# One step of a hybrid trunk: where the scan output's and the attention's tiles lie in memory

## The chip, the cores and the metric

The kernel runs on one core of a Trainium2 chip. The metric is device time of one execution in microseconds; lower is better. The core has five engines with a queue of instructions each: TensorE (PE, its weight loads PEld), VectorE (DVE), ScalarE (ACT), GpSimd (POOL) and SyncE (SP, which only issues DMAs here). Each engine works through its own queue in order and waits at an instruction until what that needs is there.

## What is computed

Two layers work on 640 tokens (512 latent, 128 context) of width 1024. A layer has one input projection whose columns go to three groups of heads: a diagonal complex scan with a gated unit (A), latent attention (B) and a gated mixing of chunks (C). Their outputs are normed, joined and projected; then comes a gated convolutional feed-forward part. The modulation of a layer is a product of SiLU(cond) with a matrix w_mod. The parts that matter here:

```python
def mixer_ssm(u, h0_re, h0_im, p):
    ...
    y = jax.nn.gelu(y).astype(u.dtype)
    y = y * jax.nn.sigmoid(y @ p['ssm_w_glu'])
...
def block_attention(q, k, v):
    ...
        s = jnp.einsum('bqhd,bkhd->bhqk', q_blk, k).astype(F32) * ATTN_SCALE
        w = jax.nn.softmax(s, axis=-1).astype(v.dtype)
        return jnp.einsum('bhqk,bkhd->bqhd', w, v)
...
def trunk_layer(x, mod, p, ctx):
    ...
    y_a, h_re, h_im = mixer_ssm(u_ssm, zeros, zeros, p)
    ...
    y_b = block_attention(q, k, v)
    y_c = mixer_gmlp(uv, p)
    x = x + gate1 * merge_heads(y_a, y_b, y_c, p['w_out_norm'], p['w_out'])
    x = x + gate2 * conv_ffn(modulate(x, shift2, scale2), p)
```

## The kernel before

All activations are held transposed (features on partitions, 642 columns: 512 latent, two of padding, 128 context). Products that need full precision are made as three products of split operands (`mm3`, lines 141 to 143).

The program is written in one order, layer by layer, and a planner at build time sets the order of the instructions in each engine's queue: an instruction written later may be put ahead of one written earlier where the planner's clock says that it is ready first. Tiles come from pools. A pool takes a stretch of the on-chip memory from one of two ends (`self.sides`, `sa` and `sb`; layer 1 swaps left and right), stacked on the pools that are open on that side, and gives it back when it closes; the program adds the waits between the users of one stretch. The order of the pools is so that of the opening and closing calls in `mixers`.

In `mixers` (from line 835) a layer's first half is written in this order. The first two blocks of the input projection give `uT`, the scan's input, in the pool `ssm` on side `sb`; it goes to DRAM and comes back as `U`. The function `scans` (line 926) runs four quarters (`ssm_quarter`), each of which writes a part of the scan's result to DRAM (`Yd`, line 781), stores the states (`ssm_states`) and calls `ssm_output`. In layer 1 `scans` is called before the chunk mixing, in layer 0 behind it. Then the pools `vt` and `prj` open on side `sa`; the rest of the projection, keys, values and queries are made there, with norms on VectorE (`key_norms`, `query_norms`; line 1163 on, line 1174 scales the queries, lines 1184 to 1189 turn those of the latent tokens in scratch tiles of `prj`). Then `prj` and `ssm` close, `yb` opens on `sa`, and `att` on `sb`, and `attention` runs.

`ssm_output` (lines 794 to 830) reads `Yd` back into `yT` with 16 DMAs, half of them from SP and half from GpSimd, and the gate's weights into `wg`; makes the GELU of two halves in `ga` and `gb` (lines 811 to 815), the gate's product (`glu`, line 824) and its sigmoid in `th`, and writes `yA` (line 830), which the merge reads later. All its tiles take over tags of the pool `ssm` (`yT` that of `U`, `wg` that of `tp`, and so on).

`attention` fills constant rows on GpSimd (lines 1214 to 1216), then handles the context heads in a pool of their own, `actx` (lines 1297 to 1344: transposes `ctr` into `qc` and `kc`, products `cmx` and maxima `nm`, scores `cs`, exponentials `Pc`, sums `co`). Among these stand `turn(0)` and `turn(1)`, which transpose the first two latent heads into `qh`, `ql`, `kh`, `kl` (lines 1223 to 1239, in `att`), and their `maxima` (`mx`, `nml`). Behind `actx` the pool `at2` opens, with the tiles `P` of the latent heads' exponentials (line 1271). Four pairs of heads follow. Between them `fill` issues steps of `mod_blocks` (lines 232 to 272): a block of w_mod is loaded from SP into one of three buffers `raw` (line 258) and multiplied (`mod`, line 261).

Of the kernel before, what the change touches and what calls it, by code (L numbers as in the profile page):

```python
# [23 lines left out]
NT = 642  # L24
# [23 lines left out]
class Trunk:  # L48
# [745 lines left out]
    def ssm_output(self, l, pool, yA):  # L794
# [3 lines left out]
        y = pool.tile([128, 2, 8, NC], F32, name=self.uid("yT"), tag="uT", bufs=1)  # L798
# [4 lines left out]
        wg = pool.tile([128, 2, 256], F32, name=self.uid("wg"), tag="tp", bufs=1)  # L803
        nc.sync.dma_start(out=wg, in_=I["ssm_w_glu"][l].rearrange("(t p) n -> p t n", t=2))
        g = [pool.tile([128, NT], F32, name=self.uid("gl"), tag=tg, bufs=1) for tg in ("E", "R")]
        for t in range(2):
            yv = y[:, t].rearrange("p i k -> p (i k)")
            nc.gpsimd.memset(g[t][:, 512:CX], 0.0)
            a = pool.tile([128, n], F32, name=self.uid("ga"), tag="m1", bufs=1)
            b = pool.tile([128, n], F32, name=self.uid("gb"), tag="m2", bufs=1)  # L810
            nc.scalar.activation(a, yv, AF.Square)
            V.tensor_scalar(a, a, 0.044715, 1.0, op0=OP.mult, op1=OP.add)
            V.tensor_tensor(a, a, yv, op=OP.mult)
            nc.scalar.activation(b, a, AF.Tanh, scale=math.sqrt(2.0 / math.pi))
            V.scalar_tensor_tensor(a, b, 1.0, yv, op0=OP.add, op1=OP.mult)
            av = a.rearrange("p (i k) -> p k i", i=8)
            for k0, k1, c in ((0, 64, 0), (65, 81, CX)):
                o = g[t][:, c:c + 8 * (k1 - k0)].rearrange("p (k i) -> p k i", i=8)
                nc.scalar.activation(o, av[:, k0:k1], AF.Copy, scale=0.5)
        for m in range(2):  # L820
# [5 lines left out]
            for s, (lo, hi) in enumerate(((0, 320), (320, NT))):  # L826
                th = pool.tile([128, 322], F32, name=self.uid("th"), tag="H", bufs=1)
# [5 lines left out]
    def mixers(self, l, M, n1, N, hh, hl, fill):  # L833
# [94 lines left out]
        def scans(tables):  # L928
            hq = ssm.tile([128, 2, 2, 2, NS], F32, name=self.uid("hq"), tag="hq")
            for q in range(4):  # L930
                self.ssm_quarter(l, q, ssm, tables or self.ssm_load(l, q, ssm), U, st, hq)
                tables = None
            self.ssm_states(l, st)
            self.ssm_output(l, ssm, yA)
# [16 lines left out]
        if l == 0:  # L951
# [4 lines left out]
            scans(None)  # L956

# [111 lines left out]
        ssm_ctx.close()  # L1069
# [4 lines left out]
        with ExitStack() as es:  # L1074
            at = es.enter_context(tc.tile_pool(name=f"att{l}", bufs=1, side=sb))
# [115 lines left out]
    def attention(self, l, M, yb, at, es, qs, ks, Vt, yB, yA, yc, ssc, fill):  # L1191
# [105 lines left out]
        with self.tc.tile_pool(name=f"actx{l}", bufs=1, side=self.sides[1]) as cx:  # L1297
# [458 lines left out]
```

## Time and profile before

| | us |
|---|---|
| median of 3 runs | 1825.25 |
| lowest and highest | 1825.23 and 1832.4 |
| the profiled execution | 1826.58 |
| its span, first to last instruction | 1824.8 |
| TensorE busy | 1694.3 (93%) |
| VectorE busy | 1156.8 (63%) |
| ScalarE busy | 679.8 (37%) |
| GpSimd busy | 312.8 (17%) |

The profile is of one execution. The table of stretches tells which engine is full where. The timeline lists an engine's instructions with their start, length, line, tiles, and in square brackets how long the engine had sat idle before and what ended that. Layer 0's first half ends at some 390 us and layer 1's at some 1280 us; what lies between and behind is the feed-forward part, in which TensorE has hardly a gap.

### The profile page before, as it was taken

Reading aid. Unit: us, or ns where it says so; the run is one execution under the profiler, and the core shown is the slowest. Engines: PE = TensorE matmul, PEld = TensorE weight load, DVE = VectorE, ACT = ScalarE, POOL = GpSimd, SP = SyncE. Lnnn points to the kernel's source line nnn. Section 1 sums busy time; section 2 is a strip of 40 time slices with the busy share of each in tenths; the row PEclk is TensorE's granted clock in tenths of the full one; section 3 lists DMA queues with packets and bytes.
Section 4 is the critical chain, followed back from the end, with each engine's and each line's share of the span. In section 5 each row is a group of like instructions: output and inputs, shape, how many; then the busy total and the mean of one; then the engine's idle time right before and its main releaser. Section 6 shows DMA issues by size and latency. Waiting matters only on the chain.

```text
span 1824.8 us, 28970 instructions
## 1 busy us (share of the span) xinstructions
PE 1694.3 (93%) x11248; PEld 1512.6 (83%) x11248; DVE 1156.8 (63%) x2421; ACT 679.8 (37%) x1210; POOL 312.8 (17%) x738
## 2 busy tenths in 40 slices
PE   5878889999989999999999888999989999999998
PEld 3767755468889999999999876455989999999998
DVE  6887875667674646556477568566786464555564
ACT  4334454433452414224244346343344232332241
POOL 2886200000086060540000120000000000000000
PEclk7889789899899999999999978999989999999999
DMA  9265453301443523234132633540223131331221
GB/s 281 84 174 148 124 162 123 110 15 56 129 137 118 170 56 116 59 94 116 35 90 67 164 105 107 167 133 1 70 70 93 36 104 47 93 92 36 82 82 58
DMA packets 217577, 182.48 MB, mean 100 GB/s; under 512 B 33438, under 2 KB 202204, under 8 KB 217440
## 3 DMA queue, kind: packets, MB, share of 16 engines
q1 hardware_dynamic: 194736, 154.33, 28.2%
q0 software_dynamic: 8272, 23.87, 4.4%
q10 hardware_dynamic: 14432, 2.44, 0.7%
q8 instruction: 89, 1.46, 0.3%
q14 instruction: 48, 0.39, 0.1%
HBM read 161.94 MB, written 18.64 MB: 99 GB/s over the span
## 4 chain that ended last, share of the span: by engine, by line
PE 75%; DVE 10%; DMA 7%; ACT 4%; POOL 2%; issue 2%; ACTq 1%; SPq 0%; DVEq 0%; POOLq 0%
PE up L141 11%; PE up L143 11%; PE up L142 11%; PE dn L142 6%; PE dn L141 6%; PE dn L143 6%; PE o L1287 3%; PE mod L261 2%; DMA raw<-w_mod 2%; PE wo L141 1%; PE wo L143 1%; PE wo L142 1%; DMA raw<-ffn_w_up 1%; PE s L1267 1%; PE win L141 1%
## 5 line engine op out<-in xcount | busy, mean ns | idle before, releaser
L141 PE MATMUL up<-hh,whi 128*128 128x322 f32 x1408 | 435.6, 315 | 8.8 <-ACT hh L357 7.9
L143 PE MATMUL up<-hh,wlo 128*128 128x322 f32 x1408 | 440.9, 314 | 1.1 <-DVE wlo L118 1.0
L142 PE MATMUL up<-hl,whi 128*128 128x322 f32 x1408 | 439.7, 313 | 1.6 <-DVE hl L358 1.5
L141 PEld LDWEIGHTS up<-hh,whi 128*128 128x128 f32 x1408 | 266.1, 191 | 14.3 <-ACT hh L357 7.2
L142 PEld LDWEIGHTS up<-hl,whi 128*128 128x128 f32 x1408 | 268.8, 191 | 2.6 <-DVE hl L358 2.6
L143 PEld LDWEIGHTS up<-hh,wlo 128*128 128x128 f32 x1408 | 267.9, 190 | 2.9 <-DVE wlo L118 1.9
L118 DVE TENSOR_TENSOR wlo<-raw,whi 128x1024 fp32r<-128x1024 f32 (+1 forms) x116 | 146.7, 1266 | 142.2 <-ACT whi L117 141.0
L142 PE MATMUL dn<-glo,dh 128*128 128x322 f32 (+1 forms) x704 | 218.5, 312 | 0.2 <-DVE glo L118 0.2
L143 PE MATMUL dn<-gh,dl 128*128 128x322 f32 (+1 forms) x704 | 217.9, 311 | 0.0
L141 PE MATMUL dn<-gh,dh 128*128 128x322 f32 (+1 forms) x704 | 209.4, 312 | 4.5 <-DVE xT L1501 2.9
L1501 DVE SCALAR_TENSOR_TENSOR xT<-dn,mod,xT 128x320 f32<-128x320 f32 (+2 forms) x288 | 112.2, 435 | 129.5 <-PE dn L143 129.3
L117 ACT CAST whi<-raw 128x1024 fp32r<-128x1024 f32 (+1 forms) x116 | 120.5, 1040 | 151.1 <-PE up L142 56.8
L1532 ACT ACTIVATE cv<-up,prm,cw 128x321 f32<-128x321 f32 x88 | 54.3, 619 | 252.5 <-PE up L143 252.3
L141 PEld LDWEIGHTS dn<-gh,dh 128*128 128x128 f32 x704 | 131.0, 190 | 5.3 <-DVE xT L1501 3.1
L142 PEld LDWEIGHTS dn<-glo,dh 128*128 128x128 f32 x704 | 133.2, 189 | 0.5 <-DVE glo L118 0.5
L143 PEld LDWEIGHTS dn<-gh,dl 128*128 128x128 f32 x704 | 133.5, 190 | 0.0
L1533 DVE SCALAR_TENSOR_TENSOR cv<-up,cw,cv 128x320 f32<-128x320 f32 x88 | 48.3, 549 | 67.5 <-ACT cv L1532 67.5
L261 PE MATMUL mod<-raw,sT 128*32 128x256 f32 x768 | 64.5, 431 | 27.1 <-DMA raw<-w_mod 24.8
L118 DVE TENSOR_TENSOR dl<-raw,dh 128x1024 fp32r<-128x1024 f32 x44 | 54.0, 1227 | 45.8 <-ACT dh L117 45.6
L117 ACT CAST dh<-raw 128x1024 fp32r<-128x1024 f32 x44 | 46.1, 1047 | 56.8 <-DMA raw<-ffn_w_down 50.1
L261 PEld LDWEIGHTS mod<-raw,sT 128*32 128x32 f32 x768 | 19.5, 114 | 57.5 <-DMA raw<-w_mod 29.2
L1250 DVE TENSOR_REDUCE nml<-mx 128x1 f32<-128x640 f32 x64 | 50.9, 820 | 24.0 <-PE mx L1248 23.7
(472 smaller groups left out, 3422.5 us busy)
## 6 DMA issues: line engine op xcount, KB each, us to landing
raw<-w_mod SPq DMA_DIRECT2D x96, 512.0 KB, 4.6
raw<-ffn_w_up SPq DMA_DIRECT2D x88, 512.0 KB, 4.1
raw<-ffn_w_down SPq DMA_DIRECT2D x44, 512.0 KB, 3.5
raw<-w_in SPq DMA_DIRECT2D x10, 512.0 KB, 5.7
we<-WEd POOLq DMA_DIRECT2D x8, 512.0 KB, 4.1
qt<-Qd POOLq DMA_DIRECT2D x8, 512.0 KB, 5.1
raw<-w_out SPq DMA_DIRECT2D x16, 256.0 KB, 5.1
raw<-w_out SPq DMA_DIRECT2D x8, 512.0 KB, 3.4
```

Of the source, the lines that this page charges most:

```text
L117: self.nc.scalar.copy(hi, raw)
L118: self.nc.vector.tensor_tensor(lo, raw, hi.bitcast(F32), op=OP.subtract)
L141: mm(ps, wh, xh, start=start, stop=False)
L142: mm(ps, wh, xl, start=False, stop=False)
L143: mm(ps, wl, xh, start=False, stop=stop)
L261: nc.tensor.matmul(ps[j * 32:j * 32 + 32, c0:c0 + 256], self.sT[:, k0 + j, :], rv[:, j, :], start=k0 == 0, stop=k0 == 4)
L1250: V.tensor_reduce(nm[:, tt:tt + 1], pb[:, :, :320], axis=AX.XY, op=OP.max, negate=True)
L1267: mm(ps, kh[i][:, kc_], qh[i], start=True, stop=False)
L1287: mm(pb[i * 64:(i + 1) * 64, 0], Vt[:, kt, 2 * p + i], Ps[i][kt], start=kt == 0, stop=kt == 4)
L1501: self.nc.vector.scalar_tensor_tensor(self.xT[:, m, a:b], po[:, a - lo:b - lo], self.modcol(l, gi, m, c), self.xT[:, m, a:b], op0=OP.mult, ...
L1532: A.activation(z[:, 0:321], po[:, 0:321], AF.Identity, bias=b, scale=c1)
L1533: V.scalar_tensor_tensor(z[:, 1:321], po[:, 0:320], c0, z[:, 1:321], op0=OP.mult, op1=OP.add)
```

## The change

The pool `ssm` closes at the scan's last output, before `vt` opens, not before the attention. `ssm_output` is taken out of `scans` and gets a pool of its own, `so`, on the same side, with tags of its own; its tile `gb` goes and the tanh is made in place in `ga`. In layer 1 it is thereby written behind the chunk mixing. The pools `att` and `actx` open on side `sa`, on top of `yb`; `at2` stays on `sb`.

```diff
@@ ssm_output
-        y = pool.tile([128, 2, 8, NC], F32, name=self.uid("yT"), tag="uT", bufs=1)
+        y = pool.tile([128, 2, 8, NC], F32, name=self.uid("yT"), tag="yT", bufs=1)
...
-        wg = pool.tile([128, 2, 256], F32, name=self.uid("wg"), tag="tp", bufs=1)
+        wg = pool.tile([128, 2, 256], F32, name=self.uid("wg"), tag="wg", bufs=1)
...
-        g = [pool.tile([128, NT], F32, name=self.uid("gl"), tag=tg, bufs=1) for tg in ("E", "R")]
+        g = [pool.tile([128, NT], F32, name=self.uid("gl"), tag=tg, bufs=1) for tg in ("g0", "g1")]
...
-            a = pool.tile([128, n], F32, name=self.uid("ga"), tag="m1", bufs=1)
-            b = pool.tile([128, n], F32, name=self.uid("gb"), tag="m2", bufs=1)
+            a = pool.tile([128, n], F32, name=self.uid("ga"), tag="ga", bufs=1)
...
-            nc.scalar.activation(b, a, AF.Tanh, scale=math.sqrt(2.0 / math.pi))
-            V.scalar_tensor_tensor(a, b, 1.0, yv, op0=OP.add, op1=OP.mult)
+            nc.scalar.activation(a, a, AF.Tanh, scale=math.sqrt(2.0 / math.pi))
+            V.scalar_tensor_tensor(a, a, 1.0, yv, op0=OP.add, op1=OP.mult)
...
-                th = pool.tile([128, 322], F32, name=self.uid("th"), tag="H", bufs=1)
+                th = pool.tile([128, 322], F32, name=self.uid("th"), tag="th", bufs=1)
@@ mixers
             self.ssm_states(l, st)
-            self.ssm_output(l, ssm, yA)
...
             scans(None)
+        ssm_ctx.close()
+        with tc.tile_pool(name=f"so{l}", bufs=1, side=sb) as so:
+            self.ssm_output(l, so, yA)
...
         prj.close()
-        ssm_ctx.close()
...
-            at = es.enter_context(tc.tile_pool(name=f"att{l}", bufs=1, side=sb))
+            at = es.enter_context(tc.tile_pool(name=f"att{l}", bufs=1, side=sa))
@@ attention
-        with self.tc.tile_pool(name=f"actx{l}", bufs=1, side=self.sides[1]) as cx:
+        with self.tc.tile_pool(name=f"actx{l}", bufs=1, side=self.sides[0]) as cx:
```

## Rows read from the trace of the kernel before

**Rows 1.** The page: busy share of TensorE; the chain that ended last, by engine.

```profile
PE 1694.3 (93%) x11248; PEld 1512.6 (83%) x11248; DVE 1156.8 (63%) x2421; ACT 679.8 (37%) x1210; POOL 312.8 (17%) x738
PE 75%; DVE 10%; DMA 7%; ACT 4%; POOL 2%; issue 2%; ACTq 1%; SPq 0%; DVEq 0%; POOLq 0%
```

**Rows 2.** Busy time by stretch: stretch, length, each engine's busy us, granted clock, DMA.

```profile
240.00:250.00 10.00, 6.29 (x58) 3.26 (x57) 9.65 (x25) 2.06 (x5) 0.00 (x0) 0.96 0.51 163
245.00:340.00 95.00, 84.64 (x566) 46.29 (x567) 58.57 (x107) 43.09 (x83) 3.27 (x6) 0.94 0.57 181
280.00:290.00 10.00, 9.04 (x64) 5.64 (x63) 7.45 (x20) 7.63 (x17) 0.00 (x0) 1.00 0.03 6
1107.00:1137.00 30.00, 23.60 (x155) 18.69 (x154) 28.45 (x73) 16.34 (x24) 2.94 (x6) 0.82 0.46 150
1160.00:1170.00 10.00, 9.65 (x68) 7.17 (x71) 8.15 (x23) 7.53 (x18) 0.00 (x0) 1.00 0.18 55
```

**Rows 3.** Timeline of GpSimd: start, length, line, tiles, idle before and its releaser.

```profile
250.67 0.52 POOL L1214 MEMSET ql<- 1x512 f32 x1 [31.83 <-DVE yA L830]
...
1075.15 1.05 POOL L800 DMA_DIRECT2D yT<-Yd  x2 [3.11 <-DMA Yd<-ys]
```

**Rows 4.** Timeline of VectorE, layer 0.

```profile
249.99 0.49 DVE L830 TENSOR_TENSOR yA<-th,gl 128x322 f32<-128x322 f32 x1
...
251.77 0.69 DVE L1189 TENSOR_TENSOR qs<-qx,qx 128x512 f32<-128x512 f32 x1
```

**Rows 5.** Timeline of ScalarE, layer 0.

```profile
250.65 1.26 ACT L1305 ACTIVATE qc<-ctr,qg 96x512 f32<-96x512 f32 x2 [1.87 <-DVE yA L830]
251.80 1.25 ACT L1236 ACTIVATE kh<-kt,kg 96x512 fp32r<-96x512 f32 x2
```

**Rows 6.** Timeline of TensorE, layer 0.

```profile
247.48 0.64 PE L261 MATMUL mod<-raw,sT 128*32 128x256 f32 x8 [2.79 <-DMA raw<-w_mod]
249.05 0.93 PE L261 MATMUL mod<-raw,sT 128*32 128x256 f32 x8 [0.93 <-DMA raw<-w_mod]
...
253.44 1.09 PE L147 MATMUL ctr<-ident,ks 128*96 128x128 f32 x4
...
256.73 2.05 PE L1313 MATMUL cmx<-kc,qc 96*128 96x128 f32 x16
...
333.39 0.64 PE L261 MATMUL mod<-raw,sT 128*32 128x256 f32 x8 [2.13 <-DMA raw<-w_mod]
```

**Rows 7.** Timeline of VectorE, layer 1.

```profile
1106.48 0.61 DVE L1154 TENSOR_SCALAR ms<-ms 128x48 f32<-128x48 f32 x1
...
1107.74 0.58 DVE L104 TENSOR_SCALAR rs_y<-rs_sh 128x48 int32<-128x48 int32 x1
...
1121.25 0.75 DVE L1237 SCALAR_TENSOR_TENSOR kl<-kt,kg,kh 96x512 fp32r<-96x512 f32 x1
...
1123.65 0.34 DVE L1237 SCALAR_TENSOR_TENSOR kl<-kt,kg,kh 96x128 fp32r<-96x128 f32 x1
...
1125.11 0.18 DVE L1154 TENSOR_SCALAR ms<-ms 128x32 f32<-128x32 f32 x1
...
1135.96 0.68 DVE L1189 TENSOR_TENSOR qs<-qx,qx 128x512 f32<-128x512 f32 x1
```

**Rows 8.** Timeline of ScalarE, layer 1.

```profile
1077.95 0.75 ACT L811 ACTIVATE ga<-yT 128x648 f32<-128x648 f32 x1 [2.02 <-DMA yT<-Yd]
...
1136.94 0.62 ACT L1354 ACTIVATE ac<-yA 128x512 f32<-128x512 f32 x1
...
1160.99 1.08 ACT L1271 ACTIVATE P<-s 128x512 f32<-128x512 f32 x2
```

**Rows 9.** Timeline of TensorE, layer 1.

```profile
1082.98 0.80 PE L1036 MATMUL kv<-whi,ckh 128*128 128x512 f32 x1 [3.19 <-ACT sq L980]
...
1213.76 0.64 PE L261 MATMUL mod<-raw,sT 128*32 128x256 f32 x8 [3.08 <-DMA raw<-w_mod]
```

**Rows 10.** Instructions on the tile `yT`: its DMAs, from issue to landing.

```profile
DMA to landing us min/median/max: 1.9/4.2/5.5
```

## The prediction

> **What bounds the kernel now.** I read the page first: TensorE is busy for 93% of the span and carries 75% of the chain that ended last [rows 1]. So an edit that adds no matmul can only win TensorE's idle time and the time it runs at the lower clock. The stretches come next [rows 2]: in layer 0 from 245 to 340 us TensorE is busy for 84.64 of 95.00 us (granted clock 0.94), and in layer 1 from 1107 to 1137 us for 23.60 of 30.00 us (0.82) while VectorE is busy for 28.45 of 30.00. That last row says who is late there: VectorE, with the norms of the queries and keys. In layer 0 the tightest ten microseconds, 240 to 250, hold 9.65 us of VectorE and 6.29 us of TensorE.
>
> Then I ask what the attention waits for. GpSimd's fill of `ql` (line 1214) reads nothing, yet it sat idle for 31.83 us until line 830, the last step of the scan output [rows 3]. `ql` belongs to the pool `att`, laid over the memory of the pool `ssm`, and line 830 reads two tiles of `ssm`. The first copy into `qc` (line 1305, pool `actx`) also starts at 250.65, right behind line 830 at 249.99 plus 0.49 us [rows 4, 5]. So the first instructions of a pool wait for the last user of the whole pool that lay there. The same is seen on the other side: line 1354 writes `ac` (pool `yb`, over the closed projection pool `prj`) at 1136.94, just behind line 1189 at 1135.96 plus 0.68 us, the last that touches `prj` [rows 7, 8].
>
> **The change part by part.** From the tile shapes in the code, in bytes of one partition: `prj` has about 31,000, `yb` 17,500, `att` 23,600. On the new side `att` stands on `yb` and covers 17,500 to 41,100, so it lies over `prj`; `actx` starts at 41,100 and lies over nothing recent. `at2` drops to the bottom of the old side, over `ssm` and the new pool `so`, both done by then. So the edit exchanges waits: `actx` loses its wait for line 830; `att` exchanges line 830 for line 1189; `at2` loses its wait for the end of the context heads; the scan output's tiles wait for the whole of `ssm`.
>
> (1) `actx`, layer 0. Its 16 transposes, copies and the `cmx` products need only the context rows, but were held to 250.65. TensorE meanwhile waits 2.79 and 0.93 us for blocks of w_mod, at 247.48 and 249.05 [rows 6]: 3.72 us together. What can fill them is the four `ctr` transposes at 253.44 (1.09 us), their twins (not shown, four more of the same) and the `cmx` products at 256.73 (2.05 us): 4.2 us of work. The queue is fixed when the program is built, so not every hole is met; I take -3.0, ends -3.7 and 0. In layer 1 the context rows themselves come late, so nothing there. The load of `kc`'s one-hot rows (line 1299) stands in SP's queue among the w_mod blocks and is set free with `actx`; it can only stop holding those behind it.
>
> (2) `att`, layer 0. Its first copy `kh` moves from 251.80 [rows 5] to behind 251.77 plus 0.69, which is 252.46 [rows 4]: 0.7 us later. The turned queries need line 1189 anyway. I take 0, ends 0 and +0.7. GpSimd has nothing queued behind its fills.
>
> (3) `att`, layer 1. Before, the copies `kl` (line 1237) were made in the middle of VectorE's chain: 0.75 and 0.34 us for a head [rows 7], 2.2 us for two. Behind line 1189 they no longer delay the norms. The six fills leave this chain too: beside them line 1154 and the two steps behind it took 0.61, 0.58 and 0.58 us (the first and the last are shown), against 0.18 for the same line later [rows 7], which is 1.2 us in all. So line 1189 ends up to 3.4 us earlier. Given back: the two long `kh` copies, 1.25 us for two as in layer 0 [rows 5], now stand behind the gate. I take -2.0; ends -3.4 (all kept) and +3.4 (chain not shortened, and `kh` with both heads' `kl` behind it: 1.25 + 2.2).
>
> (4) `at2`. In layer 1 the first exponential into `P` started at 1160.99 [rows 8], when the context heads were through. With `P` free earlier, the scores of the first pair and the context heads can fill one another's gaps. TensorE's idle there is 0.96 us (280 to 290) and 0.35 us (1160 to 1170) [rows 2]. I take -1.0, ends -1.3 and 0.
>
> (5) The pool `so`. Sixteen DMAs bring `yT`, eight from SP, eight from GpSimd, 0.53 us of issue each on the latter. Before, most of them started as soon as `U` was read; only two on GpSimd waited for the last store, up to 1075.15 in layer 1 [rows 3]. Now all wait for it. The half that line 811 reads first is four issues on each queue: 1075.2 + 2.1 = 1077.3, and with the median landing of 4.2 us [rows 10] it is there at 1081.5, where line 811 started at 1077.95 after waiting 2.02 us [rows 8]. So up to 3.5 us later. Behind line 811 on ScalarE stand the copies that release TensorE, which already idles 3.19 us at 1082.98 [rows 9]. Should the planner put those copies ahead of line 811, the wait of 2.02 us disappears instead. In layer 0 the same sum gives 0.6 us, with other work on ScalarE over it. I take 0; ends -2.0 and +4.1. Also on SP's queue the w_glu load and the first w_mod blocks come after the eight loads; those blocks lay unused until 243 in layer 0, so that costs nothing.
>
> A page has another price for the landing. The Trainium skill, "DMA: Bandwidth & Descriptors", section "Anatomy of one DMA — SWDGE (gpsimd) path", gives about 2.0 us of fixed cost for a transfer; by that estimate the upper end of (5) would be +1.4 in layer 1 and the range would lose some 2 us above. The trace says 1.9 at least and 4.2 in the middle [rows 10], so the page's figure is its best case and I keep mine.
>
> (6) What is late next: the stream of w_mod blocks that fills the attention. At its end TensorE already waits 2.13 us in layer 0 [rows 6] and 3.08 us in layer 1 [rows 9] for the last block. A gain made early in the attention lets the stream move up only as far as its three buffers are freed earlier. I give back +2.0 of the 6.0; ends 0 and +5.2 (both waits grow by all that was won ahead of them, at most the sum of the two waits).
>
> Arithmetic, tanh in place and the smaller tiles: same instructions with the same shapes, cost nothing. Sum: -3.0 + 0 - 2.0 - 1.0 + 0 + 2.0 = -4.0 us. The profiled execution took 1826.58 us (span 1824.8 and 1.78 around it), so 1822.6; it stands 1.3 above the median of 1825.25, so the prediction is 1821.3, rounded 1821.
>
> **The rivals.** *The gate only moves.* The attention of a latent head cannot begin before the queries are turned (line 1189) in either kernel, so the wait that goes was never the last one, and w_mod sets the pace. For it: VectorE is full in both stretches [rows 2] and in layer 0 line 1189 ends 2 us after line 830 [rows 4]. Against it: the 3.72 us of holes in layer 0. Time: 1825, no change (0 to -1).
>
> *The holes close altogether.* The planner lays out the whole attention anew, and context work fills most of the stalls: of the 10.36 us idle in 245 to 340 and the 6.40 us in 1107 to 1137 [rows 2], plus the 3.19 and 2.02 us around line 811. If half of the first two and all of (5)'s gain are won: -8.4 - 2.0 = about -10, 1815. Against it: w_mod's waits at the end stay.
>
> *Slower, by the pool `so`.* Line 811 stays at its place in ScalarE's queue and the data come 3.5 us later; TensorE's idle of 3.19 us at 1082.98 grows by that, and the scan output's last steps (0.49 us for each line 830 [rows 4], some 3.3 us in all with line 829) slide into the stretch in which VectorE has 1.55 us to spare. That is 3.5 + 3.3 = +6.8 us, against it (1) and (4) at half, -2 and -0.5, with 2.5 returned by w_mod: about +6.8, 1832. It decides from the point where the first half of `yT` lands later than about 1079.7, when line 811 would end in its old place plus its own slack, and where the planner did not see it.
>
> **How the numbers follow.** Forecast 0.45 (its own range 1817 to 1824.5), gate only moves 0.20, holes close 0.18, slower 0.17. Differences of 0.5%, 9.1 us, are about what a measurement of this kernel can tell from no change: below 1816.1 counts as faster, above 1834.4 as slower. Faster: the holes case and a little of the forecast's edge, 0.22. Slower: the upper third of the slower case, and (3) and (5) at their upper ends together (+7.5, with the stream's +5.2), 0.12. Same: 0.66. The range takes the holes case at 1813 and the slower case at 1833 as ends.
>
> **What would show it.** After the change: `qc` copied before 245 in layer 0 and not tied to line 830; `kh` and the fills of `ql` right behind line 1189 in both layers; the first `P` less than 2 us behind the first scores; TensorE's idle in 240 to 250 down from 3.7 to 1 us; line 1189 in layer 1 at 1133 or so; line 811 in layer 1 between 1079 and 1082, with the idle of 3.19 us smaller. Wrong would make it: `kh` well ahead of line 1189 (then memory isn't shared as I worked out), the idle at 1082.98 grown, or the two waits at the end of w_mod grown by more than 2 us together.

## The result, and the profile after

The changed kernel takes 1838.75 us in the median (1834.55 to 1844.58), the kernel before, timed beside it, 1828.88 us (1825.21 to 1832.4): a ratio of 1.0064 with an interval of 1.0050 to 1.0078. It is slower, by 9.9 us in the medians; I had forecast 4.0 us faster, 1821 with 1813 to 1833 as the range. The forecast started from 1825.25 us for the kernel before, the median of three runs, which is 3.6 us less than the median of nine here. The execution that was profiled took 1841.15 us (span 1839.3), against 1826.58 of the one before.

First the page of the changed kernel: busy time by engine, and the chain that ended last. TensorE is busy 2.2 us longer than in [rows 1] while the span grew by 14.5, so what was lost is idle time, and DMA's share of the chain rose from 7% to 8%.

```profile
PE 1696.5 (92%) x11248; PEld 1508.7 (82%) x11248; DVE 1159.3 (63%) x2421; ACT 678.8 (37%) x1210; POOL 310.0 (17%) x738
PE 73%; DVE 10%; DMA 8%; ACT 4%; issue 2%; POOL 2%; SPq 1%; ACTq 0%; DVEq 0%; POOLq 0%
```

**Layer 0.** TensorE's timeline after the change (start, length, line, tiles, idle before and its releaser; lines 810 to 829 of the changed kernel are 811 to 830 of the one before, its 981 to 1062 are 980 to 1061):

```profile
250.22 0.27 PE L147 MATMUL nmt<-ident,nm 128*8 128x128 f32 x1 [1.08 <-DVE nm L1314]
252.31 0.64 PE L261 MATMUL mod<-raw,sT 128*32 128x256 f32 x8 [1.81 <-DMA raw<-w_mod]
260.91 0.64 PE L261 MATMUL mod<-raw,sT 128*32 128x256 f32 x8 [1.67 <-DMA raw<-w_mod]
...
266.48 0.64 PE L261 MATMUL mod<-raw,sT 128*32 128x256 f32 x8 [1.02 <-DMA raw<-w_mod]
268.64 0.64 PE L261 MATMUL mod<-raw,sT 128*32 128x256 f32 x8 [0.74 <-DMA raw<-w_mod]
...
334.32 0.64 PE L261 MATMUL mod<-raw,sT 128*32 128x256 f32 x8 [1.76 <-DMA raw<-w_mod]
```

ScalarE's, VectorE's and GpSimd's timelines of the same stretch:

```profile
242.49 1.26 ACT L1305 ACTIVATE qc<-ctr,qg 96x512 f32<-96x512 f32 x2 [0.54 <-PE ctr L147]
...
256.91 1.25 ACT L1236 ACTIVATE kh<-kt,kg 96x512 fp32r<-96x512 f32 x2
```

```profile
252.49 0.49 DVE L829 TENSOR_TENSOR yA<-th,gl 128x320 f32<-128x320 f32 x1
252.89 0.68 DVE L1188 TENSOR_TENSOR qs<-qx,qx 128x512 f32<-128x512 f32 x1
253.49 0.69 DVE L1189 TENSOR_TENSOR qs<-qx,qx 128x512 f32<-128x512 f32 x1
```

```profile
254.41 0.52 POOL L1214 MEMSET ql<- 1x512 f32 x1 [31.60 <-DVE qs L1189]
```

The gates moved. `qc` no longer waits for the scan output's last step (242.49, and 250.65 in [rows 5]), and the fill of `ql` now waits for line 1189 and not for line 830 [rows 3]. (Which part of the edit moved `qc` was settled only by the experiments with either half alone, below.) But the holes of [rows 6] were not filled, they wandered: the waits for w_mod of 2.79 and 0.93 us are gone, and 1.81, 1.67, 1.02 and 0.74 us stand further on. The stretches say the same (stretch, length, busy us of PE, PEld, DVE, ACT, POOL, granted clock, DMA): TensorE's idle time in 240 to 250 fell from 3.71 to 1.52 us, in 245 to 340 it grew from 10.36 to 11.04 [rows 2].

```profile
245.00:340.00 95.00, 83.96 (x583) 45.33 (x582) 59.48 (x111) 41.44 (x82) 3.46 (x6) 0.96 0.57 178
240.00:250.00 10.00, 8.48 (x68) 6.45 (x68) 9.17 (x26) 4.52 (x9) 0.00 (x0) 1.00 0.04 8
```

**Layer 1.** TensorE after the change, from the end of the input projection to the last query product:

```profile
1090.03 2.51 PE L823 MATMUL glu<-gl,wg 128*128 128x320 f32 x4 [4.29 <-ACT gl L818]
...
1106.33 1.07 PE L261 MATMUL mod<-raw,sT 128*32 128x256 f32 x16
...
1108.61 0.40 PE L1039 MATMUL kv<-whi,ckl 128*128 128x512 f32 x1
...
1113.51 1.08 PE L261 MATMUL mod<-raw,sT 128*32 128x256 f32 x8 [3.97 <-DMA raw<-w_mod]
...
1129.25 0.44 PE L1056 MATMUL q<-whi,cqh 128*128 128x384 f32 x1 [1.52 <-ACT hsq L1062]
...
1131.29 0.34 PE L1058 MATMUL q<-whi,cql 128*128 128x384 f32 x1
```

SP's queue of the same time, and ScalarE:

```profile
1083.30 0.41 SPq L258 DMA_DIRECT2D raw<-w_mod  x1
...
1088.13 0.37 SPq L258 DMA_DIRECT2D raw<-w_mod  x1
1102.50 0.36 SPq L1023 DMA_DIRECT2D out_new_ckv<-ckt  x1
1107.03 21.12 SPq L258 DMA_DIRECT2D raw<-w_mod  x9
```

```profile
1085.09 0.74 ACT L810 ACTIVATE ga<-yT 128x648 f32<-128x648 f32 x1 [3.22 <-DMA yT<-Yd]
...
1146.35 1.25 ACT L1236 ACTIVATE kh<-kt,kg 96x512 fp32r<-96x512 f32 x2
1147.49 0.63 ACT L1354 ACTIVATE ac<-yA 128x512 f32<-128x512 f32 x1
```

This holds the longest new wait. The first two w_mod blocks are used at 1106.33 (16 products), and only then is a buffer free and the third block's load leaves SP, at 1107.03. TensorE's queue has six kv and three query products between the second block and the third; it waits 3.97 us there, until 1113.51, and the query products that feed VectorE's norms stand behind it. Before, the next loads also left SP behind the first two blocks, at 1104.79, but 21 query products lay between the second block and the third, and TensorE did not wait. Nothing in the diff touches this place: the planner, which orders each queue when the program is built, laid it out anew. The kernel before, TensorE and SP:

```profile
1104.09 1.07 PE L261 MATMUL mod<-raw,sT 128*32 128x256 f32 x16
1108.97 0.64 PE L261 MATMUL mod<-raw,sT 128*32 128x256 f32 x8
```

```profile
1104.79 1.47 SPq L258 DMA_DIRECT2D raw<-w_mod  x3
```

The length of the wait has a second part that the order does not give: the block came late. Before, the load issued at 1104.79 had landed 3.65 us later; here the products that use the block start 6.48 us after its issue (5.99 and 4.88 us in two more profiles of this kernel, with waits of 3.50 and 2.38). The stretches of the changed kernel show how it came in (columns as above; the last two are DMA's busy share of its 16 engines and GB/s):

```profile
1107.00:1111.50 4.50, 2.53 (x17) 1.60 (x9) 2.43 (x7) 3.98 (x8) 0.00 (x0) 1.00 0.68 224
1111.50:1113.50 2.00, 0.00 (x0) 0.00 (x0) 1.83 (x7) 0.00 (x0) 0.00 (x0) 0.97 0.07 17
1113.50:1115.00 1.50, 1.50 (x9) 0.69 (x10) 1.29 (x7) 0.00 (x0) 0.00 (x0) 0.50 0.04 14
```

At 224 GB/s the first stretch moved about 1.01 MB, nearly the two blocks of 512 KB that were under way; in the next 2 us only 0.07 of the 16 DMA engines' time was used, about one engine's share, and TensorE stood still for the rest. Why that rest came so late is not shown. Behind the wait TensorE's granted clock fell to 0.50, the lower of its two levels (1.2 in place of 2.4 GHz).

Two more steps of the profiled pair: where [rows 9] had 3.19 us of waiting for ScalarE ahead of the kv products, there are now 4.29 us ahead of the scan output's gate products; and the end of layer 1's attention ran at the lower clock, with the same instructions as before (1.16 us for line 371 in the first profile of the kernel before, 2.08 here). The stretch there, with its clock of 0.51, and the products:

```profile
1253.30:1260.20 6.90, 6.90 (x24) 5.35 (x23) 3.98 (x6) 1.76 (x4) 0.00 (x0) 0.51 0.00 0
```

```profile
1255.39 2.08 PE L371 MATMUL mbl<-dg,ones 128*128 128x128 f32 x8
```

The last step, in layer 0's feed-forward, lies far from everything the diff touches. VectorE, GpSimd and TensorE there:

```profile
537.12 7.52 DVE L118 TENSOR_TENSOR wlo<-raw,whi 128x1024 fp32r<-128x1024 f32 x1 [2.39 <-ACT whi L117]
```

```profile
537.17 0.47 POOL L95 TENSOR_TENSOR Tr<-Tr,tr 128x128 f32<-128x128 f32 x1
...
543.09 0.48 POOL L95 TENSOR_TENSOR Tr<-Tr,tr 128x144 f32<-128x144 f32 x1
```

```profile
545.84 0.61 PE L141 MATMUL dn<-gh,dh 128*128 128x320 f32 x1 [8.02 <-DVE cv L1541]
```

A subtraction that usually takes 1.23 us took 7.52. It began 0.05 us ahead of the first GpSimd instruction shown and ended 1.08 us behind the end of the last one of a closed row, and TensorE waited 8.02 us.

For each stretch, the median shift of the same instructions between two traces, counted from the first profile of the kernel before, gives the account (us; three profiles of the changed kernel, two of which belong to the experiments, and a second one of the kernel before):

| stretch of before | after, 1st | 2nd | 3rd | before, 2nd |
|---|---|---|---|---|
| 0 to 210 | +1.0 | +1.4 | +0.8 | +1.3 |
| 210 to 330, layer 0's attention | +0.1 | +3.8 | +3.0 | +0.7 |
| 330 to 480 | +0.3 | -2.4 | +0.7 | -3.9 |
| 480 to 600, feed-forward begins | +3.0 | -3.9 | -4.4 | +1.2 |
| 600 to 1050 | +0.3 | -0.3 | +0.2 | -0.4 |
| 1050 to 1170, layer 1 up to the attention | +5.8 | +6.8 | +6.5 | -5.2 |
| 1170 to 1260, layer 1's attention | +2.4 | +2.5 | +1.7 | +1.1 |
| 1260 to the end | +1.5 | +1.9 | +2.3 | +0.1 |

Only the rows from 1050 on carry the same sign and about the same size in all three. Of the -5.2 of the kernel before against itself, 3.4 us are a difference of the granted clock while the kv products ran (0.70 in one profile, 0.82 in the other), so layer 1 is better read from the last kv product on. That is done in this table, from TensorE's timelines: from the end of the last kv product to the end of the last query product, to the first product of the maxima (line 1248), from there to the first output product `wo`, and from the last kv product to the end of TensorE's last product.

| kernel | kv to q | kv to maxima | maxima to wo | kv to end |
|---|---|---|---|---|
| before, two profiles | 15.5, 15.5 | 37.2, 37.1 | 121.3, 119.9 | 716.9, 715.5 |
| changed, three profiles | 22.6, 23.2, 21.1 | 41.2, 42.0, 39.6 | 124.0, 125.1, 125.9 | 725.0, 727.3, 726.1 |
| new scan output, old attention pools | 22.4 | 41.8 | 121.5 | 722.7 |
| old scan output, new attention pools | 15.5 | 38.2 | 124.6 | 720.0 |
| scan output on top, new attention pools | 16.9 | 36.3 | 121.7 | 714.9 |
| scan output on top, old attention pools | 23.4 | 42.9 | 121.8 | 721.2 |
| changed, actx alone back | 16.2 | 35.6 | 120.5 | 714.4 |
| changed, no blocks in the projections | 12.5 | 35.2 | 130.8 | 722.5 |
| before, no blocks in the projections | 12.8 | 37.0 | 129.9 | 723.6 |
| on top, three steps | 14.8 | 35.8 | 123.1 | 718.2 |
| on top, three steps, rotations on VectorE | 14.8 | 35.5 | 119.1 | 714.0 |

The changed kernel loses 8 to 12 us from the last kv product to the end, as much as the median. The loss has three parts: 2.4 to 4.9 us up to the first maxima, where the wait for the third block lies, 2.7 to 6.0 from the maxima to `wo`, and 1.3 to 2.3 behind that. Of the 7.1 us between 15.5 and 22.6 in the column "kv to q", 3.97 are the wait for the block and 1.52 a wait for ScalarE's squares (1129.25 above), which in the kernel before comes only behind the last query product; most of the rest is the lower clock behind the first wait. Some 3 us of the 7 are won back ahead of the maxima.

### The profile page after: what moved, and what is told of

The parts are those of the page before. It is cut to its first block, busy times and chain, and to the rows that moved or that the text cites. A ratio compares the mean times of both kernels' runs of the same rounds, so it can differ in the third digit from the quotient of the medians.

```text
span 1839.3 us, 28986 instructions
## 1 busy us (share of the span) xinstructions
PE 1696.5 (92%) x11248; PEld 1508.7 (82%) x11248; DVE 1159.3 (63%) x2421; ACT 678.8 (37%) x1210; POOL 310.0 (17%) x738
## 4 chain that ended last, share of the span: by engine, by line
PE 73%; DVE 10%; DMA 8%; ACT 4%; issue 2%; POOL 2%; SPq 1%; ACTq 0%; DVEq 0%; POOLq 0%
PE up L141 11%; PE up L143 11%; PE up L142 10%; PE dn L141 5%; PE dn L142 5%; PE dn L143 5%; PE o L1287 3%; PE mod L261 2%; DMA raw<-w_mod 2%; PE wo L141 1%; PE wo L143 1%; PE wo L142 1%; PE s L1267 1%; DVE wlo L118 1%; DMA raw<-ffn_w_up 1%
## 5 line engine op out<-in xcount | busy, mean ns | idle before, releaser
L118 DVE TENSOR_TENSOR wlo<-raw,whi 128x1024 fp32r<-128x1024 f32 (+1 forms) x116 | 151.0, 1303 | 144.6 <-ACT whi L117 143.3
```

The costliest lines, as they stand in the source:

```text
L118: self.nc.vector.tensor_tensor(lo, raw, hi.bitcast(F32), op=OP.subtract)
```

## The experiments

**The changed kernel again, and the kernel before again.** No edit.

> The changed kernel once more, unaltered, to see which of the places where it lost time come back. In the first profile it stood 14.4 us behind the profile of before, built up in three steps: 4.0 us in layer 0's feed-forward, where one subtraction on VectorE took 7.52 us beside GpSimd's rotations; 5.5 us in layer 1 between the scan output and the attention; 2.6 us near 1255, where TensorE's granted clock read 0.51. Theory A (all of it belongs to the changed order): all three places show again within 1 us each, time 1835 to 1842. Theory B (the first and third are drawn anew in each execution): the subtraction takes 1.2 to 3.3 us and the clock near 1255 reads 1.0, or other places do it; only the 5.5 us in layer 1 shows again.

> The kernel before once more, for the spread of its own profile. Theory A (places fixed by the order): subtractions of layer 0's feed-forward stay at 1.2 to 3.3 us, granted clock near 1245 stays 1.0, time 1825 to 1830. Theory B (drawn anew): in this profile one of the subtractions beside GpSimd's rotations may take over 5 us, or a stretch near 1245 run at half the clock, with the same effect of 2 to 4 us. In layer 1 both expect what the first profile showed: line 811 near 1078 and line 1189 ending near 1136.

> The changed kernel a third time, for its profile. The subtraction of 7.52 us beside GpSimd's rotations showed in one of two profiles of it, and in none of the kernel before. If it is drawn anew in each execution: 1.2 to 3.3 us or over 5 us here, with layer 0's feed-forward 7 us apart between the two cases. The clock of 0.51 over line 371 of the merge showed in both profiles of the changed kernel and once in the others: again here if it hangs on the order. Layer 1 from the scan output to the first maxima: 5 to 7 us longer than before, as in all three profiles with the new scan output.

The first took 1835.35 us (ratio 1.0053, 1.0032 to 1.0074), the kernel before 1827.16 (1.0002, 0.9984 to 1.0020), the third profile of the changed kernel 1837.46. The long subtraction came back in neither of the two new profiles of the changed kernel, so it is drawn anew in each execution. Line 371 ran slowly in all three (2.08, 2.08 and 1.91 us; 1.16 in the first profile of before), but it did so in the next kernel too (2.04), which has the old scan output. In the second profile of the kernel before it took 1.70 us. The loss of layer 1 came back each time, which speaks for theory B in the feed-forward and for theory A in layer 1.

**Only the attention's pools moved.**

```diff
-at = es.enter_context(tc.tile_pool(name=f"att{l}", bufs=1, side=sb))
+at = es.enter_context(tc.tile_pool(name=f"att{l}", bufs=1, side=sa))
-with self.tc.tile_pool(name=f"actx{l}", bufs=1, side=self.sides[1]) as cx:
+with self.tc.tile_pool(name=f"actx{l}", bufs=1, side=self.sides[0]) as cx:
```

> The kernel before with only the attention's two pools moved to the other side; the scan output stays inside the pool of the scans, as before. My prediction's terms (1) to (4) alone: 3 to 6 us won, less 2 returned by the w_mod stream, 1822. Rival (the loss of layer 1 is the attention's new wait and the order that the planner makes of it): 1833 to 1837, with line 1189 ending 4 us or more later than before's 1136.6 and TensorE waiting about 4 us for a w_mod block ahead of the query products. Rival (the loss is the scan output's): within 2 us of before.

1831.14 us, ratio 1.0028 (1.0014 to 1.0042): neither the 1822 that my terms (1) to (4) alone give nor the 1833 of the rival. Line 1189 ended 32.3 us behind the last kv product, against 34.1 in both profiles of the kernel before, so the chain of norms is 1.8 us shorter, about what term (3) had. But ahead of the maxima TensorE now waits for VectorE, with w_mod products at the head of its queue (its timeline, below), and from the maxima to `wo` it takes 3 to 5 us longer than before.

```profile
1134.67 1.55 PE L261 MATMUL mod<-raw,sT 128*32 128x256 f32 x24 [2.44 <-DVE ql L1230]
```

In layer 0 the move of `actx` did not free `qc`. ScalarE's row, right behind the end of line 830 (249.69 plus 0.49 us):

```profile
250.35 1.26 ACT L1305 ACTIVATE qc<-ctr,qg 96x512 f32<-96x512 f32 x2 [1.64 <-DVE yA L830]
```

**Only the scan output's pool and its place.** The changed kernel with both lines above set back to the old side.

> The changed kernel with the attention's two pools back on the old side: only the scan output's pool, its place in the program and the earlier closing of the scans' pool differ from before. If the loss of layer 1 is the scan output's (yT brought 3.5 us later, its line on ScalarE late, SP's loads of w_mod pushed back): 1833 to 1837, with line 810 starting near 1085 less what is gained ahead of it, and the 3.97 us wait for w_mod ahead of the query products. If the loss is the attention's: within 2 us of before, 1827 to 1831, with line 810 still late but no such wait.

1835.77 us in four runs, ratio 1.0062 (1.0037 to 1.0087), as much as the whole change. It has both of the changed kernel's new waits, 5.25 us for `gl` and 3.66 us for the third w_mod block. And `qc` is free in it, with both pools of the attention on the old side. ScalarE's row, then TensorE's:

```profile
242.38 1.26 ACT L1305 ACTIVATE qc<-ctr,qg 96x512 f32<-96x512 f32 x2 [0.54 <-PE ctr L147]
```

```profile
1105.11 0.64 PE L261 MATMUL mod<-raw,sT 128*32 128x256 f32 x8 [3.66 <-DMA raw<-w_mod]
```

So the scan output's half brings the stall of layer 1 and the larger part of what is lost there: from the last kv product to the end it loses 5.8 to 7.2 us, the attention's half alone 3.1 to 4.5, the whole change 8 to 12. Which of its two waits it is, and whether the memory under the pool or the order of the queue makes it, was the next question.

**The scan output's pool off the memory of the scans.**

```diff
-        with tc.tile_pool(name=f"so{l}", bufs=1, side=sb) as so:
-            self.ssm_output(l, so, yA)
...
         pj = prj.enter_context(tc.tile_pool(name=f"prj{l}", bufs=1, side=sa))
+        with tc.tile_pool(name=f"so{l}", bufs=1, side=sa) as so:
+            self.ssm_output(l, so, yA)
```

> The changed kernel with the scan output's small pool on the attention's side, on top of the projections' pool, so that it no longer lies over the memory of the scans. If the late yT is what costs (its sixteen loads wait for the last user of the scans' pool, the new_ssm stores): line 810 starts 2 to 4 us earlier against the tail of the projections, TensorE's wait of 4.3 to 5.3 us for gl falls below 3, and the time is 4 to 6 us below the changed kernel's, 1830 or so. If the wait for gl is only the order in which TensorE's queue was laid out (glu ahead of kv): the wait stays above 4 us and the time within 2 us of the changed kernel's.

1830.6 us, ratio 1.0005 (0.9990 to 1.0020): the loss is gone, from the last kv product to the end as well (714.9 us), and not for the reason that I had given. Line 810 waits for `yT` as long as in the changed kernel: GpSimd's half of the loads now waits for a step of the projections (line 982 on ScalarE), SP's half leaves 0.09 us behind the landing of the last store to `Yd`. The wait for `gl` is 4.29 us as in the changed kernel. ScalarE's row:

```profile
1086.64 0.74 ACT L810 ACTIVATE ga<-yT 128x648 f32<-128x648 f32 x1 [3.23 <-DMA yT<-Yd]
```

So the late `yT` is not what costs. What changed is TensorE's queue: 24 query products again lie between the second block and the third, and the longest wait for a block among them is 0.58 us:

```profile
1109.27 1.07 PE L261 MATMUL mod<-raw,sT 128*32 128x256 f32 x16
1116.67 0.64 PE L261 MATMUL mod<-raw,sT 128*32 128x256 f32 x8 [0.58 <-DMA raw<-w_mod]
```

**The same, with the attention's pools back on the old side.** The two lines of the pools as in the first diff, set back.

> The scan output's small pool on the attention's side, off the memory of the scans, and both pools of the attention back on the old side. TensorE's queue in layer 1 has the order of the changed kernel again: two w_mod blocks, kv, 3 query products, a block, 3 query products, a block. If the order costs: wait of 3 to 4 us for w_mod ahead of the query products, line 1189 late by 4 to 6 us, time 1834 to 1838. If the memory under the scan output costs: as the kernel with the pool on top, 1828 to 1831.

1833.21 us, ratio 1.0038 (1.0014 to 1.0062), with the order of the changed kernel and its waits. The time lies between the ranges of the two theories and decides nothing; the wait, and line 1189 (39.7 us behind the last kv product, 34.1 in the kernel before), are those of the theory that the order costs. TensorE's timeline, first the last kv and the last query product, then the third block:

```profile
1099.02 0.40 PE L1040 MATMUL kv<-whi,ckl 128*128 128x512 f32 x1
...
1122.46 0.34 PE L1059 MATMUL q<-whi,cql 128*128 128x384 f32 x1
```

```profile
1103.79 1.08 PE L261 MATMUL mod<-raw,sT 128*32 128x256 f32 x8 [3.84 <-DMA raw<-w_mod]
```

**actx alone back on the old side**, from the changed kernel.

```diff
-with self.tc.tile_pool(name=f"actx{l}", bufs=1, side=self.sides[0]) as cx:
+with self.tc.tile_pool(name=f"actx{l}", bufs=1, side=self.sides[1]) as cx:
```

> The changed kernel with the context's pool actx alone back on the old side; att stays on the new one, the scan output keeps its small pool over the memory of the scans. In the program as built TensorE's queue then has the first two w_mod blocks behind all kv products, 24 query products, and only then the third; in the changed kernel the third stands 3 query products behind the second. If the wait for that third block is what costs (order): no wait above 2 us ahead of the query products, line 1189 ends 4 to 6 us earlier against the kv products than in the changed kernel, time 1828 to 1831. If the scan output's pool over the scans costs (memory): still there, so 1835 to 1839.

1830.03 us, ratio 1.0025 (1.0006 to 1.0044). The scan output lies over the scans' memory as in the changed kernel, and the wait of 3.97 us is gone with the order. TensorE's w_mod products, then the last kv and query product:

```profile
1101.24 1.07 PE L261 MATMUL mod<-raw,sT 128*32 128x256 f32 x16
1107.45 1.17 PE L261 MATMUL mod<-raw,sT 128*32 128x256 f32 x16
```

```profile
1100.91 0.40 PE L1039 MATMUL kv<-whi,ckl 128*128 128x512 f32 x1
...
1117.21 0.34 PE L1058 MATMUL q<-whi,cql 128*128 128x384 f32 x1
```

From the last kv to the last query product it takes 16.2 us, with the same products in it as the changed kernel's 22.6. The two pairs go in opposite directions: moving the pools back brings the third block forward in one, and moving one of them back sends it off in the other. The wait, and the loss up to the maxima, go with the place of the block and not with a pool. (The last gate product changes its place along with the block, so these pairs alone do not single the block out; the next experiment takes it away.) In the median this form is still 3.2 us above the kernel before, though from the last kv product to the end it loses nothing (714.4 us). (My expectation counted 3 query products between the blocks of the changed kernel; with the kv products it is nine.) The profiled execution, 1822.88 us, was the shortest of ten, though VectorE's timeline shows that it had the long subtraction in the feed-forward:

```profile
532.02 7.66 DVE L118 TENSOR_TENSOR wlo<-raw,whi 128x1024 fp32r<-128x1024 f32 x1 [2.85 <-ACT whi L117]
```

**No blocks in layer 1's projections**, in the changed kernel and in the kernel before.

```diff
-        for _ in range(5):
+        for _ in range(5 if l == 0 else 0):
             next(fill, None)
```

> The changed kernel without the w_mod blocks that are handed out at the end of layer 1's projections (five steps of the stream); they follow in the attention instead. If the wait of 3.5 to 4.0 us for a w_mod block ahead of the query products is a third of the loss: line 1189 ends 3 to 5 us earlier against the kv products, and the time is 2 to 4 us below the changed kernel's, 1831 to 1833. If VectorE's chain of norms sets line 1189 whatever TensorE waits: same place within 1 us, and the blocks put off lengthen the attention's end, 1836 to 1842.

> The kernel before without the five steps of the w_mod stream at the end of layer 1's projections: its TensorE waits nowhere above 0.5 us for those blocks among the query products, so nothing is to be had there, and the five blocks lengthen the attention behind. If taking them out only removes the stall of the changed kernel: 0 to 3 us slower than before, 1827 to 1830. If blocks among the query products cost of themselves (VectorE's share of them, ScalarE's copies): 2 to 5 us faster, 1822 to 1825.

From the changed kernel 1830.25 us (1.0013, 1.0000 to 1.0027), from the kernel before 1829.44 (1.0022, 1.0006 to 1.0039). The maxima begin 4.3 to 6.8 us sooner after the last kv product than in the changed kernel, but only 0.2 us sooner in the kernel before, where there was no stall. And the blocks put off come back: from the maxima to `wo` it is 130.8 and 129.9 us, 5 to 10 us more than with them in their place. From the last kv product to the end 2.5 to 4.8 us are left of the gain (722.5 us). The whole time gained more, some 7 us against the changed kernel's 1.0053; its profile stood 1.6 us ahead of before's by 1050, those of the changed kernel 5.0 behind, 0.9 ahead and 0.1 behind, which the edit does not explain. With the stall gone the next wait on TensorE's timeline is for ScalarE's squares of the queries:

```profile
1116.95 0.75 PE L147 MATMUL kt<-ident,ks 128*96 128x128 f32 x5 [3.43 <-ACT hsq L1062]
```

**Three steps in place of five, with the pool on top**, and then with the rotations of layer 1's tables on VectorE.

```diff
-        for _ in range(5):
+        for _ in range(5 if l == 0 else 3):
```

```diff
-hooks[4] = [lambda: self.ssm_rotations(l + 1, tb[0], nc.gpsimd, 2)]
+hooks[4] = [lambda: self.ssm_rotations(l + 1, tb[0], nc.vector, 2)]
```

> The kernel with the scan output's pool on top, with three steps of the stream at the end of layer 1's projections in place of five, so that two query groups of 24 and 36 products run with two pairs of blocks ahead of them and none further on. Were it the sum of the two mended forms (1830.6 and 1830.3, each within 0.3% of before): about 2 us below either, 1826 to 1829, the same as before or just under it. If the blocks put off come back at the attention's end: 1830 to 1833.

> The last form (scan output's pool on top, three steps of the stream) with the rotations for layer 1 made on VectorE in place of GpSimd. In two of nine profiles with the new scan output a subtraction on VectorE took 7.5 and 7.7 us while GpSimd ran its rotations, and layer 0's feed-forward was then 6 to 7 us longer than in the others. If that meeting is the cause: no subtraction of 1024 columns above 3.3 us there, and the time is 0 to 2 us below the last form's 1826.8, as the mean share of such executions is worth, so 1824.5 to 1827, with the slowest executions gone. If VectorE has no room for them in the feed-forward: TensorE waits for VectorE there and the time is 3 to 6 us above, 1830 to 1833.

1826.79 us (1.0004, 0.9989 to 1.0020) and 1828.41 (1.0012, 0.9993 to 1.0031): level with the kernel before. With the rotations on VectorE no long subtraction showed, but VectorE is busy for 85.08 us in 480 to 600 in place of 69.33, and TensorE waited 2.5 and 1.6 us there for the split of the feed-forward's activations. The first form beats the kernel before in nothing that can be measured. The second is 1.6 us above the first in the median, between its two expected ranges and within the noise, and its slowest execution (1838.06) is not gone.

## Why the prediction was wrong, step by step

**(1), actx in layer 0: forecast -3.0, nothing was won (the stretch 210 to 330 came 0.1 to 3.8 us longer).** The gate went and `qc` started 8 us earlier, but not by the part that I had named: with `actx` alone moved, `qc` still stands 0.17 us behind line 830, and with the scan output's half alone it starts at 242.38. So the claim that `actx` on the new side lies over nothing recent does not hold while the scans' pool is open; what ties it there is not shown. And none of the 3.72 us of holes was won. The waits for w_mod in 235 to 300 sum to 5.2 us before, to 5.2, 5.5 and 6.4 us in the three profiles of the changed kernel, and to 7.0 and 5.3 with the pools' half and the scan output's half alone. That fits my rival in which the gate only moves: the stream of blocks sets the pace there, and context work laid into a hole ahead of a block leaves another hole behind it. The failed step is that I priced a hole by the work that fits into it, and didn't ask when the next block lands.

**(2), att in layer 0: forecast 0 to +0.7, too small.** `kh` starts at 256.91, 2.7 us behind the end of line 1189 (254.18), and line 1189 itself ends 1.7 us later than in [rows 4], 1.0 of which the trace was late by 210 already; a step of the scan output (line 829, 0.49 us) now stands in its chain. Both are places in a queue, which I had not counted.

**(3), att in layer 1: forecast -2.0, and right as far as it goes.** The copies `kl` and the fills left the chain, and `kh` stands right behind line 1189 (ends 1146.21, `kh` at 1146.35). From the last query product to line 1189 it takes 14.6 us, against 18.5 before. To the first maxima it is 18.6 against 21.7, a gain of 3.1 us. Part of it is not the pools': with the old pools and the new scan output the first of these is 16.3. With the blocks out of the projections in both, the changed kernel reaches the maxima 1.7 us sooner than the kernel before (35.2 against 37.0), which is the size that I had forecast. Line 1189 did not come at 1133, because the query products had come 7 us late.

**(4), at2: forecast -1.0, not seen in layer 1 and not singled out in layer 0.** The first exponential follows the first scores after 3.6 us in layer 0 (8.4 before), but after 7.2 in layer 1 (1164.54 to 1171.73; 7.6 before), not within 2 us.

**(5), the pool of the scan output: forecast 0 with ends -2.0 and +4.1; the mechanism was right, and it is small.** Line 810 started at 1085.09; the trace was 5.0 us behind by 1050, so that is 1080.1 in the old count, inside my 1079 to 1082. `yT` took 2.2, 3.5 and 4.7 us from issue to landing (least, median, most). The page that I had weighed against the trace, the Trainium skill's "DMA: Bandwidth & Descriptors", section "Anatomy of one DMA — SWDGE (gpsimd) path", has about 2.0 us as the fixed part; here too that was the least and not the median. TensorE's wait here grew from 3.19 to 4.29 us (up to 5.25 in the form without the new pools), but the last kv product came only 0.5 to 4.3 us later after the input projection (23.3 to 23.7 us, against 22.8 and 19.4). The kernel with the pool on top has that wait too and loses nothing in all.

**(6), the w_mod stream: the step that failed.** I looked at it at the end of each attention only, where the waits are no longer than they were (2.13 and 3.08 us before; 1.76, 0.96 and 2.37 after). For SP's queue I wrote that the blocks behind the eight loads cost nothing, from layer 0 alone, and in layer 1 I took the order of TensorE's queue as given wherever the diff does not reach. The planner put nine short products between the second block and the third in place of 21 query products. The block took 6.5 us from its issue (1107.03) to the products that use it (1113.51), and nine products, some 2.2 us of work, do not cover that; even the 3.65 us of the kernel before would not have been covered. This term was +2.0 and, with layer 1's projections in it, would have had to be +5.5 to +7.7 (21.1 to 23.2 against 15.5 us from kv to the last query product), of which term (3) gives some 3 back. With (1) at nothing, that turns the -4.0 into a loss of 2.5 to 4.7. The rest of the measured 9.9 us lies mostly between the maxima and `wo`, where I had no term that could grow except this stream's waits, and these did not; what made it longer stays open (below).

**The rivals.** "Slower by the pool so" had the sign and 1832, and half of the mechanism: TensorE's idle grew ahead of the gate products, by 1.1 us and not 3.5, and the scan output's tail did not slide into VectorE's full stretch but ended sooner after the input projection (22.0 us, against 26.5 and 23.2 in the two profiles of before). The missing part was the block. The chance of 0.12 for slower was low for a reason that I can name: I let the ends of the terms add up, and a term that isn't in the list has no end.

**What stays open.** The attention of layer 1 from the maxima to `wo` is 3 to 5 us longer in the changed kernel and in the one with the new pools alone. In the profiled pair 2.6 us of it is TensorE's clock near 1255, with the same instructions ahead of it; but line 371 took about 2 us in the kernel with only the new scan output, in the one with the pool on top and in the one with `actx` back as well, whose stretches are no longer than before's (120.5 to 121.7 us). So the clock does not tell the kernels with the long stretch from the others, and what sets it there was not settled. Nor was the +3.0 and +3.8 of layer 0's attention in two of three profiles traced to one instruction.

## What to carry to other kernels

A change of memory in a kernel whose queues are ordered by a planner can change every queue, also where no line was touched; compare the order of the bounding engine's instructions before working out which waits go. A background stream must be priced by the distance in its consumer's queue from the instruction that frees a buffer to the one that uses the next block, against the time from issue to landing (here 4.9 to 6.5 us in three executions of one kernel, so not the best case); here taking it out of a busy stretch gave the stall back, and the blocks cost about as much again where they were put. And when an edit has two halves, build each alone before saying which wait went by which.

## What the runs showed of the hardware

**VectorE can be held for a whole row of GpSimd instructions.** The Trainium skill, "SBUF — State Buffer", section "SBUF: two separate sides", says that a VectorE instruction with two inputs in SBUF and a GpSimd instruction that reads SBUF exclude each other, and that whichever starts first holds the port for the whole instruction. The trace agrees that one of them stands still: beside VectorE's subtractions in the kernel before, between 530 and 545 us, five of GpSimd's steps took 1.00 to 1.62 us, where steps of the same shapes otherwise took 0.2 to 0.74. Four subtractions of 1024 columns there began while a GpSimd step ran and took 1.23 to 1.31 us, little or no longer than usual, and GpSimd's next step was the one held up. But it can also lose for a whole row: the subtraction of 7.52 us ran from 537.12 to 544.64, again with a GpSimd step running at its start (line 94, 536.81 to 537.23), and thirteen more instructions of GpSimd are recorded in that time, from 537.17 to 543.57, none of them held up. The same was seen once more (7.66 us, again thirteen), and on a smaller scale in the kernel before (3.29 us beside six steps, at 519.29). What decides between the two outcomes is not shown. The long form showed in two of the nine profiles with the new scan output and GpSimd's rotations, and layer 0's feed-forward was then 5 to 8 us longer than in the other seven (515.6 us against 508.1 to 510.9).

**A block can hang on one DMA engine.** At the stall of the changed kernel two blocks of 512 KB came in at 224 GB/s up to 1111.5, and then the DMA engines' busy share was 0.07 (17 GB/s) for 2 us until TensorE could go on; in the second profile it was 0.07 as well from 1104.5 to 1106.0. The median block of that kernel takes 4.7 us from issue to landing, this one 6.5.

**The lower clock follows a wait and outlasts it.** Behind the wait for ScalarE ahead of the kv products the same products took 0.63 us in place of 0.40, at a granted clock of 0.70 over the stretch in one execution of the kernel before and 0.82 in another, and the stretch was 22.8 and 19.4 us long. The wait was 3.19 us in both; in the first the products ran at the lower level for some 14 us behind it, in the second for some 3.5 us and, later, for 3.5 more. That alone is 3.4 us between two executions of one kernel, as much as the terms that I was adding.
